# Four-sublayer trunk on one core: the DeltaNet stage with ScalarE and VectorE in program order, later weight splits, and its modulation sums made one stage earlier

## The chip, the core and the metric

One core of a Trainium2 chip runs the whole kernel. Its engines are TensorE (PE in the rows), VectorE (DVE), ScalarE (ACT), GpSimd (POOL) and SyncE (SP), which here only issues DMAs. The metric is the device time of one execution in microseconds (us).

## What is computed

A trunk of four sublayers on x (512 tokens x 1024): a mixer of pooling and sparse attention ("e"), a gated feed-forward with a depthwise convolution ("f"), a gated DeltaNet ("o") and a second feed-forward. Each is wrapped in a modulation from the vector c (shift, scale and gate, each a 1024x1024 matrix times silu(c)) and a post-norm:

```python
def adaln_post_norm(x, c, mod_w, mod_b, ln_g, ln_b, sublayer):
    mod = jax.nn.silu(c) @ mod_w + mod_b
    shift, scale, gate = jnp.split(mod[:, None, :], 3, axis=-1)
    y = sublayer(x * (1.0 + scale) + shift)
    return layer_norm(DEEPNORM_ALPHA * x + gate * y, ln_g, ln_b)
```

The DeltaNet projects to q, k, v, gate, beta and decay, convolves q, k and v over 4 tokens, applies SiLU, normalizes q and k, and solves for each chunk of 64 tokens a triangular system:

```python
    a = jnp.einsum('bhncd,bhnsd->bhncs', kb, k) * dec_strict
    t_mat = lax.linalg.triangular_solve(a + eye, jnp.broadcast_to(eye, a.shape),
                                        left_side=True, lower=True, unit_diagonal=True)
    u = t_mat @ (v * beta[..., None])
    w = t_mat @ (kb * jnp.exp(gc)[..., None])
    attn = jnp.einsum('bhncd,bhnsd->bhncs', q, k) * dec_incl
```

A scan over the chunks, a gated norm and the output projection follow.

## The kernel before

All matrices are float32. A weight tile is split into two fp32r halves (`split`, lines 94 to 99): ScalarE rounds it to the high half (line 97), VectorE or GpSimd subtracts that from the raw tile (line 98). Each product is three matmuls (lines 103 to 105), so one projection of 128 output columns over 1024 inputs is 24 matmuls of 128x512.

The DeltaNet input stage (`odd`) walks over 33 tiles of its input projection: 16 columns for beta and decay, then `ORDER`: g0 to g4, k0 to k7, q0 to q3, g5, q4 to q7, v0 to v7, g6, g7. The generator `projs` yields the result buffer of one tile after the other. It keeps `AHEAD` tiles loaded and split in advance: after tile n's projection it issues load and split of tile n + 3. For each k, q and v tile the stage does a convolution (`conv`: line 1003 on ScalarE, three steps of line 1005 on VectorE) and a SiLU (line 1006), and starts a generator for what follows. `pump` advances every started generator by one step (to its next `yield`):

- `k_chain`: transposes (line 1021), sums of squares (1026), a power on GpSimd (1057), the decayed k (1043), and the block of A (matmul 1050, VectorE 1052), which goes to DRAM.
- `q_chain`: the same squares and power, one step later the scores q k^T (matmul 1076, VectorE 1078, mask on GpSimd 1079).
- `v_chain`: transposes and a product with beta (1065).
- `invert`: inverts all 32x32 diagonal blocks of all heads at once on VectorE. It reads A's blocks back from DRAM, then does 31 steps of a product (line 1096) and a subtraction (1097), a `yield` after every fifth, and a copy (1100), and writes the inverse and its transpose to DRAM (1101, 1102). It starts at q2.
- `y_chain`, four of them, started at the tiles in `YS`: load inverted blocks (1119) and put them together to 64-row inverses (matmuls 1124, 1131, 1139, 1141, 1148).
- `side`: the gate row of this sublayer from its finished sum (`mod_gate`), x times gain plus bias of the previous norm (`affine`, eight GpSimd instructions, lines 506 and 510), and the shift and scale of the next feed-forward (`mod_gb`).

A modulation vector is made by `mod_acc`, not by matmuls: blocks of 128 of the 1024 input rows are loaded (line 267) and added up as row times c, on VectorE (lines 276, 278) or by ScalarE's product and GpSimd's sum (270, 272). `sum_rows` then sums over the partitions (transposes 300, reduction 301). In the DeltaNet stage this is 32 loads of 256 KB, half of them summed on VectorE, half on ScalarE and GpSimd. The gate's sum of the DeltaNet is made in the down phase of the feed-forward before it (`sums`), from 16 such loads.

What sets the order: TensorE's instructions of the input stage stand in program order (`manual_schedule(engines={PE})`). ScalarE, VectorE, GpSimd and SyncE take the order that a list scheduler gives them there, by its own estimate of when operands are ready. `QUIET` names the tiles whose lower weight half VectorE computes instead of GpSimd (q5, q6, q7, v0). PSUM holds four "main" buffers (projections), three "chain" and one "side".

Of the kernel before, what the change touches and what calls it, by code (L numbers as in the profile page):

```python
# [14 lines left out]
P = 128  # L15
S = 512
D = 1024
# [9 lines left out]
class Trunk:  # L27
# [79 lines left out]

    def load_w(self, src, c0, n=P, lo_eng=None, tags=("wh", "wl")):
# [3 lines left out]
        return self.split(raw, [P, KC, n], *tags, lo_eng)  # L112
# [43 lines left out]
    def projs(self, src, tiles, h, start=None, lo_eng=None):  # L156
# [31 lines left out]
        AHEAD = 3 if self.kind == "o" else 2  # L188
        eng = lambda n: lo_eng[n] if isinstance(lo_eng, list) else lo_eng
        ahead = [self.load_w(src, *t, eng(first + n)) for n, t in enumerate(tiles[first:first + AHEAD])]  # L190
        for t, w, p in zip(tiles, ws, pss):
            if start is None:
                self.proj(p[:t[1]], w, h, slice(S // 2, S))
            yield p[:t[1]]
        for n in range(first, len(tiles)):
# [3 lines left out]
            if n + AHEAD < len(tiles):  # L199
                ahead.append(self.load_w(src, *tiles[n + AHEAD], eng(n + AHEAD)))  # L200
# [52 lines left out]
    def mod_acc(self, i, j, tag=None):  # L253
# [6 lines left out]
        acc = self.b("acc", [P, D])  # L260
        for k in range(KC):
            c = self.cs[:, k:k + 1]
            n = D if tag == "g4" else 512
            for q in range(D // n):
                part = acc[:, q * n:(q + 1) * n]
# [14 lines left out]
        return acc  # L280

    def mod_cols(self, i, j):

        nc = self.nc
        acc = yield from self.mod_acc(i, j)
        for _ in range(self.LAG[self.kind]):
            yield
        o = self.s([P, KC], f"modc{j}")
        for q in range(2):
            self.sum_rows(acc[:, q * 512:(q + 1) * 512], o[:, 4 * q:4 * q + 4])  # L290
            yield
# [11 lines left out]
    def mod_gb(self, i):  # L303

        nc = self.nc
        sc = yield from self.mod_cols(i, 1)
        sh = yield from self.mod_cols(i, 0)
# [11 lines left out]
    def mod_gate(self, i, acc=None):  # L319
# [3 lines left out]
        keep = acc is not None  # L323
        if not keep:
            acc = yield from self.mod_acc(i, 2)
        for q in range(2):
            row, part = self.b("mr", [1, 512]), acc[0:1, q * 512:(q + 1) * 512]
# [3 lines left out]
        for h in range(2):  # L331
            part = acc[:, h * 512:(h + 1) * 512]
# [3 lines left out]
            yield  # L336
            p = self.ps("side")
            nc.tensor.matmul(p, self.ones, hi, start=True, stop=False)
            nc.tensor.matmul(p, self.ones, lo, start=False, stop=True)
            if keep:  # L340
                row = self.b("mr", [1, 512])
                nc.scalar.activation(row, p[0:1], AF.Copy)
                nc.sync.dma_start(self.gate_d[:, h * 512:(h + 1) * 512], row)
            else:
                nc.scalar.activation(g[:, h * 512:(h + 1) * 512], p, AF.Copy)
        self.gate = g

    def sums(self, i):

        self.ahead = yield from self.mod_acc(i, 2, "t")  # L350

    def side(self, i):

        if self.ahead is not None:
            yield from self.mod_gate(i, self.ahead)
            self.ahead = None
            yield from self.affine(i)
            if i + 1 < len(self.subs):
                yield from self.mod_gb(i + 1)
# [7 lines left out]
        if i + 1 < len(self.subs):  # L367
            yield from self.mod_gb(i + 1)
# [145 lines left out]
    def ffn(self, i, l, h):  # L514
# [4 lines left out]
        self.go(self.side(i), 2)  # L519
        av = []  # L520
        tiles = self.tiles("f")
        for (c0, _), p in zip(tiles, self.projs(a["f_w_up"][l], tiles, h, self.begin)):
# [7 lines left out]
            if len(av) == 2:  # L530
# [3 lines left out]
                av = []  # L534
                self.pump()
# [10 lines left out]
        if i + 1 < len(self.subs) and self.subs[i + 1][0] == "o":  # L546
            self.go(self.sums(i + 1))
# [335 lines left out]
    def odd(self, i, l, h):  # L883
# [199 lines left out]
        def invert():  # L1083
# [7 lines left out]
            nc.vector.memset(Xs.rearrange("p i j -> p (i j)")[:, ::33], 1.0)  # L1091
            for j in range(31):
# [5 lines left out]
                if j % 5 == 4:  # L1098
                    yield
# [238 lines left out]
```

## Time and profile before

| | us |
|---|---|
| median of 3 runs | 1333.46 (1326.49 to 1335.98) |
| profiled execution | 1331.74 |
| its span, first to last instruction | 1329.6 |
| TensorE busy | 1253.8 (94%) |
| VectorE busy | 835.4 (63%) |
| ScalarE busy | 591.0 (44%) |
| GpSimd busy | 365.2 (27%) |

Mean granted clock of TensorE: 0.971 of full speed. The page's first section gives the busy sums, its second the busy share in 40 slices. A window gives the same for a stretch of time. A row of waits names the instruction that stood, what released it, and how long the engine was idle in all. Times count from the start of the span. The first feed-forward's up phase is about 255 to 505 us, its down phase to 605; the DeltaNet's input stage is about 605 to 881, its recurrence and output projection end at about 1000.

### The profile page before, as it was taken

The page shows a single profiled execution, that of the slowest core. Times are in us where ns is not written, and L with a number is a line of the kernel's source. Part 1 is how long each engine was busy: PE and PEld are TensorE (multiplying, and loading weights), DVE is VectorE, ACT ScalarE, POOL GpSimd, SP SyncE. Part 2 cuts the span into 40 slices and gives each one's busy share as a digit, 9 for nine tenths or more (in the row PEclk, how much of TensorE's full clock was granted, in tenths as well). Part 3 has the DMA queues.
Part 4 walks back from the last instruction along what each step waited for, and adds up shares of the span by engine and source line. Part 5 has one row for each costly group of instructions (what it writes and reads, how often), then busy time and mean ns, then how long its engine had stood idle before and what let it go on. Part 6 is the DMA issues. An engine that isn't in the chain of part 4 may idle for free. (4 is left out here: it accounts for less than half of the span.)

```text
span 1329.6 us, 17388 instructions
## 1 busy us (share of the span) xinstructions
PE 1253.8 (94%) x6359; PEld 1026.5 (77%) x6359; DVE 835.4 (63%) x1388; ACT 591.0 (44%) x1085; POOL 365.2 (27%) x308
## 2 busy tenths in 40 slices
PE   4998899899999999999989987999999999999997
PEld 3756465798888888888878866888798888888885
DVE  4589963476776777445567895537547765556328
ACT  3564756653433343326665434344555343334220
POOL 4367476340100001003585355200380010000001
PEclk9989798999999999999999998999899999999999
DMA  9952444234554536331557537573234643323311
GB/s 265 237 166 88 159 130 140 80 99 158 174 174 145 188 130 203 121 88 33 168 180 215 134 96 204 141 254 115 75 101 141 212 121 96 95 79 111 95 64 64
DMA packets 223626, 184.19 MB, mean 139 GB/s; under 512 B 24735, under 2 KB 191852, under 8 KB 223542
## 3 DMA queue, kind: packets, MB, share of 16 engines
q1 hardware_dynamic: 223542, 183.09, 45.8%
q8 instruction: 50, 0.82, 0.3%
q14 instruction: 34, 0.28, 0.1%
HBM read 169.29 MB, written 13.64 MB: 138 GB/s over the span
## 5 line engine op out<-in xcount | busy, mean ns | idle before, releaser
L103 PE MATMUL main<-h,wh 128*128 128x512 f32 (+2 forms) x1104 | 414.5, 380 | 2.2 <-ACT h L446 2.1
L104 PE MATMUL main<-h,wh 128*128 128x512 f32 (+2 forms) x1104 | 413.2, 375 | 1.9 <-DVE h L394 1.1
L105 PE MATMUL main<-h,wl 128*128 128x512 f32 (+2 forms) x1104 | 412.8, 375 | 0.0
L97 ACT ACTIVATE wh<-wr 128x1024 fp32r<-128x1024 f32 x176 | 184.3, 1050 | 316.0 <-PE main L104 213.5
L98 DVE TENSOR_TENSOR wl<-wr,wh 128x1024 fp32r<-128x1024 f32 x130 | 175.8, 1354 | 176.1 <-ACT wh L97 176.1
L103 PEld LDWEIGHTS main<-h,wh 128*128 128x128 f32 (+1 forms) x1104 | 207.7, 189 | 43.0 <-ACT h L446 2.7
L104 PEld LDWEIGHTS main<-h,wh 128*128 128x128 f32 (+1 forms) x1104 | 208.1, 189 | 40.5 <-DVE h L394 2.0
L105 PEld LDWEIGHTS main<-h,wl 128*128 128x128 f32 (+1 forms) x1104 | 208.0, 188 | 37.4 <-issue 0.4
L527 DVE SCALAR_TENSOR_TENSOR t<-main,cw,t 128x511 f32<-128x511 f32 (+1 forms) x164 | 121.6, 744 | 2.3 <-ACT t L525 0.3
L98 POOL TENSOR_TENSOR wl<-wr,wh 128x1024 fp32r<-128x1024 f32 (+1 forms) x46 | 110.3, 2402 | 45.9 <-ACT wh L97 36.3
L480 POOL TENSOR_TENSOR rstd<-rstd,mhalf 128x1 f32<-128x1 f32 x16 | 10.4, 652 | 363.4 <-DVE rstd L479 333.1
L329 POOL TENSOR_TENSOR acc<-acc,mr 1x512 f32<-1x512 f32 x8 | 12.6, 1582 | 295.8 <-DVE acc L278 222.8
L272 POOL TENSOR_TENSOR acc<-acc,mr 128x512 f32<-128x512 f32 x56 | 74.3, 1329 | 56.3 <-ACT mr L270 53.5
L270 ACT ACTIVATE mr<-mr,cs 128x512 f32<-128x512 f32 x56 | 40.2, 720 | 57.8 <-DMA mr<-in_f_mod_w_dram 39.0
L525 ACT ACTIVATE t<-main,cb,cw 128x512 f32<-128x512 f32 x82 | 62.2, 760 | 0.0
L1005 DVE SCALAR_TENSOR_TENSOR t<-main,ocw,t 128x511 f32<-128x511 f32 (+2 forms) x72 | 53.6, 744 | 3.1 <-ACT t L1003 2.1
L532 ACT ACTIVATE t<-t 128x512 f32<-128x512 f32 x42 | 26.4, 629 | 60.6 <-DVE t L527 60.6
L103 PE MATMUL main<-wh,h 128*128 128x512 f32 x128 | 50.2, 392 | 0.0
L104 PE MATMUL main<-wl,h 128*128 128x512 f32 x128 | 50.1, 391 | 0.0
L105 PE MATMUL main<-wh,h 128*128 128x512 f32 x128 | 49.8, 390 | 0.0
L394 DVE TENSOR_TENSOR h<-chain,h 128x256 fp32r<-128x256 f32 x48 | 19.4, 418 | 30.1 <-ACT h L393 29.6
L390 ACT ACTIVATE chain<-chain,B,G 128x128 f32<-128x128 f32 x84 | 33.2, 435 | 10.0 <-PE chain L382 9.5
(392 smaller groups left out, 2119.4 us busy)
## 6 DMA issues: line engine op xcount, KB each, us to landing
wr<-in_f_w_up_dram SPq DMA_DIRECT2D x84, 512.0 KB
wr<-in_f_w_down_dram SPq DMA_DIRECT2D x42, 512.0 KB
mr<-in_f_mod_w_dram SPq DMA_DIRECT2D x64, 256.0 KB
wr<-in_o_w_in_dram SPq DMA_DIRECT2D x32, 512.0 KB
g<-in_e_mod_w_dram SPq DMA_DIRECT2D x32, 256.0 KB
g<-in_f_mod_w_dram SPq DMA_DIRECT2D x16, 512.0 KB
g<-in_o_mod_w_dram SPq DMA_DIRECT2D x16, 512.0 KB
wr<-in_e_w_in_dram SPq DMA_DIRECT2D x11, 512.0 KB
```

The costliest lines, as they stand in the source:

```text
L97: nc.scalar.activation(hi, src, AF.Copy)
L98: (lo_eng or nc.vector).tensor_tensor(lo, src, hi.bitcast(F32), op=ALU.subtract)
L103: inst = mm(ps, l[0], r[0], start=start, stop=False)
L104: mm(ps, l[0], r[1], start=False, stop=False)
L105: mm(ps, l[1], r[0], start=False, stop=stop)
L270: inst = nc.scalar.activation(r, raw, AF.Copy, scale=c)
L272: nc.gpsimd.tensor_tensor(part, part, r, op=ALU.add)
L390: nc.scalar.activation(t[:, c, :], t[:, c, :], AF.Identity, scale=G[:, k:k + 1], bias=B[:, k:k + 1])
L525: nc.scalar.activation(t, p, AF.Identity, bias=cb[:, n:n + 1], scale=cw[:, 4 * NF + n:4 * NF + n + 1])
L527: nc.vector.scalar_tensor_tensor(t[:, k:], p[:, :S - k], cw[:, 2 * NF * (2 - k) + n:2 * NF * (2 - k) + n + 1], t[:, k:], op0=ALU.mult, op1 ...
L532: nc.scalar.activation(av[0], av[0], AF.Silu)
L1005: nc.vector.scalar_tensor_tensor(t[:, k:], p[:, :S - k], cw[:, 24 * (3 - k) + n:24 * (3 - k) + n + 1], t[:, k:], op0=ALU.mult, op1=ALU.add)
```

## The change

1. In the input stage ScalarE and VectorE are in program order too. GpSimd and SyncE stay with the scheduler.
2. `projs` splits a weight tile one tile later than before, two tiles ahead instead of three, but issues its raw load one tile before the split (`raw_w`).
3. The SiLU of a tile is written after `pump`, except for k0 and k1. Before, it stood ahead of it.
4. `QUIET` is q4 to q7. `YS` is v0, v2, v4, v6, with one more `yield` between the loads and the first matmul of a `y_chain`.
5. `invert` starts at q3 and takes six steps: the setup, then pieces of 10, 7, 7 and 7 inversion steps (the last with the copy), at the pumps of g5, q4, q5 and q6.
6. No modulation sum is left in the stage. The DeltaNet's gate row is finished in the up phase of the feed-forward before (8 more sums of 128x1024, `side` at 2 or 3 steps a pump), and the scale and shift sums of the next feed-forward are made in its down phase (32 loads of 256 KB and 32 sums of 128x512 on VectorE, where 16 stood). In the stage itself `side` only transposes and reduces them at g4, k0, k1 and k2, and does `affine`.

```diff
-    LAG = {"e": 1, "f": 1, "o": 3}
-    QUIET = [("q", 5), ("q", 6), ("q", 7), ("v", 0)]
-    YS = [("v", 1), ("v", 3), ("v", 5), ("v", 6)]
+    QUIET = [("q", 4), ("q", 5), ("q", 6), ("q", 7)]
+    YS = [("v", 0), ("v", 2), ("v", 4), ("v", 6)]
...
-        AHEAD = 3 if self.kind == "o" else 2
+        AHEAD, ROOM = 2, int(self.kind == "o")
         eng = lambda n: lo_eng[n] if isinstance(lo_eng, list) else lo_eng
         ahead = [self.load_w(src, *t, eng(first + n)) for n, t in enumerate(tiles[first:first + AHEAD])]
+        raws = [self.raw_w(src, *t) for t in tiles[first + AHEAD:first + AHEAD + ROOM]]
...
             self.proj(p[:m], ahead.pop(0), h)
-            if n + AHEAD < len(tiles):
-                ahead.append(self.load_w(src, *tiles[n + AHEAD], eng(n + AHEAD)))
+            if n + AHEAD + ROOM < len(tiles):
+                raws.append(self.raw_w(src, *tiles[n + AHEAD + ROOM]))
+            if raws:
+                raw = raws.pop(0)
+                ahead.append(self.split(raw, list(raw.shape), "wh", "wl", eng(n + AHEAD)))
             yield p[:m]
...
-                if kind == "e" or kind == "o" and q:
+                if kind == "e":
                     r = part if k == 0 else raw
                     inst = nc.scalar.activation(r, raw, AF.Copy, scale=c)
...
     def sums(self, i):
 
-        self.ahead = yield from self.mod_acc(i, 2, "t")
+        sc = yield from self.mod_acc(i, 1, "t")
+        sh = yield from self.mod_acc(i, 0, "t", "c")
+        self.ahead = (sh, sc)
 
     def side(self, i):
 
-        if self.ahead is not None:
-            yield from self.mod_gate(i, self.ahead)
-            self.ahead = None
+
+        nxt = i + 1 if i + 1 < len(self.subs) else None
+        if self.subs[i][0] == "o":
+            if nxt is not None:
+                yield from self.mod_gb(nxt, self.ahead)
             yield from self.affine(i)
-            if i + 1 < len(self.subs):
-                yield from self.mod_gb(i + 1)
             self.gate = self.b("gate", [P, D])
...
+        if self.before_o(i):
+            yield from self.mod_gate(nxt, True)
...
-                if j % 5 == 4:
+                if j in (9, 16, 23):
                     yield
...
-        with self.tc.manual_schedule(engines={mybir.EngineType.PE}):
+        todo = []
+        E = mybir.EngineType
+        with self.tc.manual_schedule(engines={E.PE, E.Activation, E.DVE}):
...
                     conv(hd * P, p, qh(hd))
-                    silu()
                     self.go(q_chain(hd))
-                    if hd == 2:
+                    if hd == 3:
                         self.go(invert())
...
                 self.pump()
+                if (kind, hd) not in self.ORDER[5:7]:
+                    silu()
```

Line numbers after the change are higher by 17 in the functions of the stage (1003 is 1020, 1096 is 1114).

Two places of the new order. First ScalarE, before, around the splits for the last q and the first v tiles (L97 is a weight split, L1003 the start of a convolution, L1026 the squares, L1006 the SiLU of the tile whose buffer is named t):

```order
L97 ACTIVATE wh_1234_6732<-wr_1233_6730 128x1024
L1003 ACTIVATE t_1212_6595<-main_1207_6563,ocw_5107 128x512
L1026 ACTIVATE junk_79,ssq_985_5123<-chain_1220_6623 128x128 x4
L97 ACTIVATE wh_1242_6789<-wr_1241_6787 128x1024
L1003 ACTIVATE t_1225_6665<-main_1221_6634,ocw_5107 128x512
L1026 ACTIVATE junk_79,ssq_985_5123<-chain_1231_6694 128x128
L1006 ACTIVATE g4_1211_6594<-t_1212_6595 128x512
L1026 ACTIVATE junk_79,ssq_985_5123<-chain_1231_6694 128x128 x3
L1006 ACTIVATE g4_1211_6594<-t_1225_6665 128x512
L97 ACTIVATE wh_1252_6857<-wr_1251_6855 128x1024
L1003 ACTIVATE t_1236_6736<-main_1232_6705,ocw_5107 128x512
```

And in the change, the same place (L1020, L1043 and L1023 are those lines now; wh_1243 is the weight of v1, wh_1251 that of v2, g4_1231 holds q6 and q7):

```order
L97 ACTIVATE wh_1229_6652<-wr_1214_6583 128x1024
L1020 ACTIVATE t_1232_6657<-main_1227_6625,ocw_5208 128x512
L1043 ACTIVATE junk_79,ssq_1022_5224<-chain_1240_6686 128x128 x4
L1023 ACTIVATE g4_1231_6656<-t_1232_6657 128x512
L97 ACTIVATE wh_1243_6725<-wr_1228_6650 128x1024
L1020 ACTIVATE t_1245_6729<-main_1241_6698,ocw_5208 128x512
L1043 ACTIVATE junk_79,ssq_1022_5224<-chain_1248_6744 128x128 x4
L1023 ACTIVATE g4_1231_6656<-t_1245_6729 128x512
L97 ACTIVATE wh_1251_6783<-wr_1242_6723 128x1024
L1020 ACTIVATE t_1253_6787<-main_1249_6756,ocw_5208 128x512
L1043 ACTIVATE junk_79,ssq_1022_5224<-chain_1256_6801 128x128 x4
```

Before, the split wh_1242 stood ahead of the SiLU of t_1212, whose convolution had been started earlier; now each split stands behind the SiLU of the tile before.

Second, VectorE, before, near the end of the inversion (L1096 and L1097 the inversion, L1005 a convolution, L1056 the input of a power):

```order
L1096 TENSOR_TENSOR c_1215_6608<-xn_1140_6237,xn_1141_6238 128x156
L1005 SCALAR_TENSOR_TENSOR t_1225_6665<-main_1221_6634,ocw_5107,t_1225_6665 128x510
L1097 TENSOR_TENSOR xn_1141_6238<-xn_1141_6238,c_1215_6608 128x6x26
L1056 TENSOR_SCALAR fq_990_5128<-ssq_985_5123 128x4
L1005 SCALAR_TENSOR_TENSOR t_1225_6665<-main_1221_6634,ocw_5107,t_1225_6665 128x509
L1096 TENSOR_TENSOR c_1216_6611<-xn_1140_6237,xn_1141_6238 128x135
L1097 TENSOR_TENSOR xn_1141_6238<-xn_1141_6238,c_1216_6611 128x5x27
L1096 TENSOR_TENSOR c_1217_6614<-xn_1140_6237,xn_1141_6238 128x112
L1097 TENSOR_TENSOR xn_1141_6238<-xn_1141_6238,c_1217_6614 128x4x28
L1096 TENSOR_TENSOR c_1218_6617<-xn_1140_6237,xn_1141_6238 128x87
L1097 TENSOR_TENSOR xn_1141_6238<-xn_1141_6238,c_1218_6617 128x3x29
L1096 TENSOR_TENSOR c_1219_6620<-xn_1140_6237,xn_1141_6238 128x60
```

And in the change, at its end (L1115 the inversion's last subtraction, L1118 the copy, L1022 the convolutions of q7 and then v0, L1095 the scores of q4):

```order
L1114 TENSOR_TENSOR c_1238_6677<-xn_1177_6386,xn_1178_6387 128x60
L1115 TENSOR_TENSOR xn_1178_6387<-xn_1178_6387,c_1238_6677 128x2x30
L1114 TENSOR_TENSOR c_1239_6680<-xn_1177_6386,xn_1178_6387 128x31
L1115 TENSOR_TENSOR xn_1178_6387<-xn_1178_6387,c_1239_6680 128x31
L1118 COPY xn_1177_6386<-xn_1178_6387 128x1024
L1073 TENSOR_SCALAR fq_1027_5229<-ssq_1022_5224 128x4
L1022 SCALAR_TENSOR_TENSOR t_1245_6729<-main_1241_6698,ocw_5208,t_1245_6729 128x511
L1022 SCALAR_TENSOR_TENSOR t_1245_6729<-main_1241_6698,ocw_5208,t_1245_6729 128x510
L1022 SCALAR_TENSOR_TENSOR t_1245_6729<-main_1241_6698,ocw_5208,t_1245_6729 128x509
L1206 SCALAR_TENSOR_TENSOR c2_1024_5226<-br2_1025_5227,ex_1020_5222 128x32
L1095 TENSOR_TENSOR c_1247_6740<-chain_1246_6735,g4_1034_5243 128x512
L1073 TENSOR_SCALAR fq_1027_5229<-ssq_1022_5224 128x4
```

Before, the steps of a convolution lie between single inversion instructions; now a whole piece with the copy stands ahead of q7's convolution, and the scores of q4 behind that.

## Rows read from the trace of the kernel before

**Rows 1.** Section 2 of the page: TensorE, busy tenths in 40 slices of 33.24 us.
```profile
PE   4998899899999999999989987999999999999997
```
**Rows 2.** Windows, feed-forward stage before: start:end us, length, busy us and instructions by engine.
```profile
260.00:500.00 240.00, 240.00 (x1178) 203.44 (x1178) 167.33 (x205) 101.47 (x137) 26.26 (x15) 1.00 0.46 150
505.00:600.00 95.00, 95.00 (x425) 78.78 (x424) 48.43 (x55) 30.97 (x39) 6.74 (x5) 1.00 0.42 127
```
**Rows 3.** Waits of TensorE, 640 to 884 us: line, releaser, us, times, longest.
```profile
PE side L300 <- DVE modc L301: 4.7, 1, 4.7
PE chain L1021 <- ACT junk L1026: 4.5, 2, 3.9
PE chain L1124 <- issue: 4.0, 1, 4.0
PE chain L1050 <- DVE rk L1056: 3.3, 1, 3.3
PE chain L1076 <- DVE c L1078: 1.8, 2, 1.2
PE chain L1021 <- DVE g L1052: 1.3, 1, 1.3
```
**Rows 4.** Windows of 10 us in the DeltaNet input stage (after POOL: clock, DMA share, GB/s).
```profile
690.00:700.00 10.00, 7.25 (x35) 6.68 (x36) 9.51 (x22) 5.49 (x19) 7.42 (x9) 0.83 0.73 218
760.00:770.00 10.00, 10.00 (x47) 8.28 (x46) 9.77 (x17) 2.15 (x3) 5.04 (x3) 1.00 0.30 82
770.00:780.00 10.00, 6.06 (x27) 5.04 (x26) 9.70 (x19) 5.29 (x15) 4.25 (x3) 0.83 0.38 103
800.00:810.00 10.00, 5.27 (x30) 5.13 (x29) 7.71 (x14) 4.19 (x12) 7.85 (x6) 0.66 1.00 201
830.00:840.00 10.00, 10.00 (x38) 8.45 (x38) 4.13 (x5) 2.56 (x4) 4.94 (x4) 0.67 0.69 185
```
**Rows 5.** Groups by line, 640 to 884 us: instructions, busy, mean ns, idle before.
```profile
L278 DVE SCALAR_TENSOR_TENSOR acc<-mr,cs,acc 128x512 f32<-128x512 f32 x14 | 16.6, 1189 | 29.5 <-DMA mr<-in_f_mod_w_dram 29.4
L270 ACT ACTIVATE mr<-mr,cs 128x512 f32<-128x512 f32 x14 | 10.1, 722 | 31.3 <-DMA mr<-in_f_mod_w_dram 25.2 <-DVE t L1005 3.4 <-DMA g<-xt_d 2.7
```
**Rows 6.** Timeline of VectorE: start us, us, instruction.
```profile
756.87 2.47 DVE L1097 TENSOR_TENSOR xn<-xn,c 128x231 f32<-128x231 f32 x1
763.28 0.42 DVE L1097 TENSOR_TENSOR xn<-xn,c 128x252 f32<-128x252 f32 x1
```
**Rows 7.** Timeline of GpSimd: start us, us, instruction, idle before.
```profile
663.57 7.11 POOL L510 TENSOR_TENSOR x<-x,acc 128x1024 f32<-128x1024 f32 x3 [4.67 <-DMA acc<-in_f_ln_b_dram]
...
756.54 2.54 POOL L98 TENSOR_TENSOR wl<-wr,wh 128x1024 fp32r<-128x1024 f32 x1
```
**Rows 8.** Timeline of ScalarE, the SiLU of q5.
```profile
771.80 0.63 ACT L1006 ACTIVATE g<-t 128x512 f32<-128x512 f32 x1 [7.14 <-DVE t L1005]
```
**Rows 9.** Groups of VectorE by line, 738 to 800 us.
```profile
L1096 DVE TENSOR_TENSOR c<-xn,xn 128x31 f32<-128x31 f32 (+15 forms) x31 | 16.8, 541 | 4.3 <-DMA xn<-a_d 3.4
L1097 DVE TENSOR_TENSOR xn<-xn,c 128x31 f32<-128x31 f32 (+15 forms) x31 | 16.7, 538 | 0.7
L1005 DVE SCALAR_TENSOR_TENSOR t<-main,ocw,t 128x509 f32<-128x509 f32 (+2 forms) x20 | 14.9, 747 | 1.8 <-ACT t L1003 1.6
L1078 DVE TENSOR_TENSOR c<-chain,g 128x512 f32<-128x512 f32 x7 | 4.8, 682 | 0.0
L1100 DVE COPY xn<-xn 128x1024 f32<-128x1024 f32 x1 | 1.7, 1687 | 0.0
```
**Rows 10.** Timeline of TensorE: first matmul of g5 and of q4.
```profile
739.00 0.48 PE L103 MATMUL main<-h,wh 128*128 128x512 f32 x1
...
745.81 0.48 PE L103 MATMUL main<-h,wh 128*128 128x512 f32 x1
```
**Rows 11.** Line 278: its instructions, ns least, median and most.
```profile
L278 DVE SCALAR_TENSOR_TENSOR acc<-g,cs,acc x28: 1270/1277/1286, 324.4 to 1066.7; 128x1024 f32<-128x1024 f32 x28
L278 DVE SCALAR_TENSOR_TENSOR acc<-t,cs,acc x14: 739/745/752, 497.3 to 516.8; 128x512 f32<-128x512 f32 x14
```

More of the change, by code (lines that the diff above doesn't have):

```diff
@@ L259, in mod_acc @@
         tag = tag or ("g4" if kind == "f" else "mr")
-        acc = self.b("acc", [P, D])
+        if into == "acc":
+            acc = self.b("acc", [P, D])
+            parts = [acc[:, q * 512:(q + 1) * 512] for q in range(2)]
+        else:
+            parts = [self.b(into, [P, 512]) for _ in range(2)]
         for k in range(KC):
             c = self.cs[:, k:k + 1]
-            n = D if tag == "g4" else 512
-            for q in range(D // n):
-                part = acc[:, q * n:(q + 1) * n]
+            whole = tag == "g4"
+            for q, part in enumerate([acc] if whole else parts):
+                n = D if whole else 512
                 raw = self.b(tag, [P, n])
                 nc.sync.dma_start(raw, w[k * P:(k + 1) * P, j * D + q * n:j * D + (q + 1) * n])
-                if kind == "e" or kind == "o" and q:
+                if kind == "e":
                     r = part if k == 0 else raw
@@ L279, in mod_acc, with mod_cols @@
             yield
-        return acc
-    def mod_cols(self, i, j):
+        return parts
+    def mod_cols(self, i, j, parts=None):
         nc = self.nc
-        acc = yield from self.mod_acc(i, j)
-        for _ in range(self.LAG[self.kind]):
+        if parts is None:
+            parts = yield from self.mod_acc(i, j)
             yield
@@ L317, in mod_gb, with mod_gate @@
         self.GB = (G, B)
-    def mod_gate(self, i, acc=None):
+    def mod_gate(self, i, keep=False):
         nc = self.nc
         kind, l = self.subs[i]
-        keep = acc is not None
-        if not keep:
-            acc = yield from self.mod_acc(i, 2)
+        parts = yield from self.mod_acc(i, 2)
         for q in range(2):
-            row, part = self.b("mr", [1, 512]), acc[0:1, q * 512:(q + 1) * 512]
+            row, part = self.b("mr", [1, 512]), parts[q][0:1]
             nc.sync.dma_start(row, self.a[kind + "_mod_b"][l:l + 1, 2 * D + q * 512:2 * D + (q + 1) * 512])
@@ L330, in mod_gate @@
         g = None if keep else self.b("gate", [P, D])
-        for h in range(2):
-            part = acc[:, h * 512:(h + 1) * 512]
+        for q, part in enumerate(parts):
             hi, lo = self.b("mr", [P, 512], F32R), self.b("mr", [P, 512], F32R)
@@ L366, in side @@
             self.params()
-        if i + 1 < len(self.subs):
-            yield from self.mod_gb(i + 1)
+        if nxt is not None:
+            yield from self.mod_gb(nxt)
+        if self.before_o(i):
+            yield from self.mod_gate(nxt, True)
     def new_h(self):
@@ L545, in ffn @@
         late = []
-        if i + 1 < len(self.subs) and self.subs[i + 1][0] == "o":
-            self.go(self.sums(i + 1))
+        if self.before_o(i) and i + 2 < len(self.subs):
+            self.go(self.sums(i + 2))
         for j in range(len(gs)):
```

44 lines of the change are left out of this document (23 added, 21 removed).

## The prediction

> **What bounds the kernel now.** I read the page's 40 slices first, then the waits of TensorE, then the windows around each wait, then the timelines of VectorE and GpSimd. The reader is to see in the slices that TensorE is at nine tenths or more nearly everywhere, and that outside the first stage it falls to eight and seven tenths only in slices 21, 24 and 25 (665 to 698 and 765 to 831 us) [rows 1]. In the windows both feed-forward stages have TensorE busy for every microsecond: 240.00 of 240 in the up phase before the DeltaNet stage, 95.00 of 95 in its down phase, at clock 1.00, with VectorE at 167 of 240 and 48 of 95 [rows 2]. There only more TensorE work, or a partner that becomes late, changes the time. The DeltaNet input stage (640 to 884 us) is different: TensorE waits there for 19.6 us in the eight waits of the six kinds shown, and for about 1 us in smaller ones [rows 3]. After the long ones the granted clock of the 10 us window is 0.83, 0.83, 0.66 and 0.67 [rows 4], so part of it ran at 1.2 instead of 2.4 GHz. The shortfall from 1 times 10 us is 1.7, 1.7, 3.4 and 3.3 us; a part of the third falls into the wait itself, so I count 9 us. What the stage can give back in all is thus 20 + 9, about 29 us.
>
> **The change, part by part.** I take it as four terms against the profiled execution's own 1331.74 us (its span is 1329.6).
>
> *Term A, the k heads: -5.5.* The waits of 3.3 us (a squared-norm scale that came late, behind ScalarE's work on modulation loads) and 1.3 us, and the clock of 690 to 700 (1.7 us) belong here [rows 3, 4]. The 16 modulation products on ScalarE and their adds on GpSimd leave the stage: 14 instructions of 0.72 us with 31 us of idle before them stand in one group [rows 5]. With them go the waits, since ScalarE now keeps program order, and ahead of the squares it has a weight split and a convolution start, no modulation work. That returns 6.3. What can be late instead: the weight halves of k3 and k4 are still split on GpSimd, behind three products x times gain that take 7.1 us and start only when a norm row has landed [rows 7]. There I allow 0 to 2 us and take 0.8.
>
> *Term B, the matrix inversion and the q heads: +4.* Here I count the row of VectorE by hand from the end of q3's projection (t = 0). A tile costs TensorE 6.81 us (from one first matmul to the next) [rows 10]; so without waits it would have q7 done at 33, v0 at 40, v1 at 46 and v2 at 53. VectorE's row, now in fixed order, is from t = 9.8 (first inversion piece, once the conv of q3 and a split are done): the 62 inversion instructions, 33.5 us in two groups [rows 9], less what seven of them were held, five at about 2.4 instead of 0.4 and two at 1.3 (one of the seven and a clean one are shown [rows 6]), so 22.5; the closing copy, 1.7 [rows 9]; convolutions of q4 to q7, 12 at 0.75, 9.0 [rows 9]; two weight splits, at 1.3 by the same 128x1024 row, 2.6; three score products at 0.68, 2.0 [rows 9]; and holds. An inversion instruction that meets a GpSimd split waits it out: the 128x231 subtract took 2.47 us where the 128x252 one took 0.42, and a GpSimd split ran from 756.54 to 759.08 [rows 6, 7]. In the new order two such splits (v0, v1) and one or two of GpSimd's mask products still fall beside inversion pieces: 6 us. Sum 44; so q4's score product is done near t = 55.
>
> The Trainium skill, page "SBUF — State Buffer", section "Who interferes with whom", says this as a rule: a VectorE instruction with two SBUF inputs and a GpSimd instruction that reads SBUF exclude each other for a whole instruction. The trace agrees, 2.47 against 0.42 us. By that rule moving four splits to VectorE removes holds, and it speaks against leaving v0's and v1's splits on GpSimd.
>
> TensorE against that: q7 ends at 33 as before. v0's lower half is split by GpSimd at 36, a wait of 2.4; v0 ends at 41.5. Its pump then needs a score buffer whose squares stand on ScalarE behind the SiLU of q6, which waits for q6's convolution (t = 44, behind the third inversion piece): TensorE goes on at about 47, 5.8 later. v1 follows, and v2 needs the split that stands on ScalarE behind the SiLU of q7, whose convolution is only through at 54.8, so v2 starts at 59 and ends at 65 to 66 (some 3 us of clock loss lie inside it). Before, VectorE was equally full (9.7 of 10 in 760 to 780 us [rows 4]), ScalarE waited 7.14 us for a convolution there [rows 8], and TensorE lost 4.5 + 1.8 us in waits and 1.7 in clock [rows 3, 4], 8 us, which puts the end of v2 at t = 53 + 8 = 61. So this term is a loss of 4 to 5; I take 4. Its bounds are -6 (the lag of VectorE is swallowed by the two tiles that are split ahead) and +12 (every one of v0 to v2 waits in full, at the low clock).
>
> *Term C, the v and gate heads: -13.* The waits of 4.7 (transposes of a sum whose reduction came last) and 4.0 us (triangular products whose inputs SyncE issued late, behind modulation loads) stand here, with clocks 0.66 and 0.67 [rows 3, 4]. All 32 modulation loads, 8 MB, leave the stage, as do 14 VectorE sums that idled 29.5 us for them [rows 5]. 8.7 us of waits and 5.6 of clock go: 14.3. What comes in place: the loads of the inverse's blocks now stand on SyncE behind the store of q5's scores, which by the row above is ready only near t = 62, when TensorE wants them at 65. I allow 0 to 5 and take 1.3, nearer to nothing, since the 3 us between 62 and 65 are there for the load.
>
> *Term D, the feed-forward stage before: +0.5.* It gets 8 more sums of 1.28 us in its up phase and 16 more of 0.74 in its down phase [rows 11]: 10 us to VectorE's 167 of 240 and 12 to its 48 of 95 [rows 2]. Both stay under TensorE, which hides them, and the loads, 8 MB more, meet a DMA share of 0.46 and 0.42 [rows 2]. If that cover fails (a weight split behind two sums) it costs one sum at a time; bounds 0 to 5, and I take 0.5. The recurrence and everything after it keep their order.
>
> Sum: -5.5 + 4 - 13 + 0.5 = -14, so 1331.7 - 14 = 1317.7, say 1318 us. The profiled execution lies 1.7 below the median of the three runs, inside their spread of 9.5; I leave the forecast on its scale.
>
> **The rivals.**
>
> *Everything comes back.* Split-ahead tiles and the four main result buffers swallow VectorE's lag. For it: TensorE was at 10.00 of 10 in 760 to 770 us while VectorE was already at 9.77 [rows 4], so a lag of a tile or so costs nothing. Against it: 22 us of lag (55 - 33) is three tiles, and only two are split ahead. With B at -6, C at -14 and D at 0 it gives 1306.
>
> *Program order eats it.* Term B at +12 and the late blocks at 5 us: -5.5 + 12 - 9 + 0.5 = -2, so 1330, no change that a measurement of this kernel can tell; about 1% is what it can. For it: in fixed order a SiLU that waits blocks the next weight split, which the scheduler was free to put first (in the rows of ScalarE's order above it does so once).
>
> *Slower.* The same mechanism without slack: every split of q6 to v2 stands behind a SiLU that stands behind an inversion piece, so that TensorE pays VectorE's full row from q4 on, 44 us over four tiles or 11 for one, instead of 6.81 [rows 10]. The lag of 22 us (55 - 33) turns into waits at four or five places, each with a clock loss of 1.7 to 3.4 [rows 4], about 10 more; less the 8 lost there before that is +24, and with A only half found and D at +5 the sum is -3 + 24 - 9 + 5 = +17, 1349. It decides from the point where q6's projection already waits for its split. Against it: q4 to q7 are split by VectorE right between the pieces, not after them.
>
> **How the numbers follow.** Forecast (1309 to 1324) 0.5; everything back 0.15; eaten 0.25; slower 0.1. The forecast lies close to the bound of 1% (1320), so 0.37 of its 0.5 counts as faster and 0.13 as the same: with the others faster 0.52, same 0.38, slower 0.1. The range takes in the first rival and most of the second: 1304 to 1338.
>
> **What would show it right or wrong.** In the stage's waits of TensorE the kinds of 4.7, 4.0 and 3.3 us should be gone; there should be no modulation loads or sums between 640 and 880. A new wait of 4 to 7 us should stand at v0's pump, for ScalarE's squares, and one of 2 to 4 before v2's projection, for a split. VectorE should be above nine tenths for some 45 us from q4 to v0, and the closing copy should end near 52 us after q3's projection. The feed-forward stage should stay at 100% of TensorE. If v0 and v1 pass without those waits, B is wrong and the first rival holds; if TensorE waits for splits as early as q6, the third; if the feed-forward stage shows idle time, D is.

## The result and the profile after

The changed kernel takes 1317.62 us in the median of 4 runs (1314.80 to 1322.84), the kernel before beside it 1331.92 us (4 runs, 1326.49 to 1335.98). The ratio is 0.99, with a 95% interval of 0.985 to 0.9949. The forecast was 1318. The profiled execution of the changed kernel is the longest of its four, 1322.84 us with a span of 1320.8, so the two traces lie 8.8 us apart and the medians 14.3.

The page's slices of the changed kernel, TensorE and its granted clock:

```profile
PE   4998999899999999999999989999999999999997
PEclk9999598999999999999999999989899999999998
```

Slices 21 and 25, at eight and seven tenths before [rows 1], are at nine; slice 24 is still at eight. The waits of TensorE in the changed kernel, 640 to 900 us (line, releaser: us, times, longest):

```profile
PE chain L1038 <- ACT junk L1043: 4.6, 1, 4.6
PE chain L1038 <- ACT g L1023: 1.8, 1, 1.8
PE main L105 <- DVE wl L98: 1.7, 1, 1.7
PE chain L1038 <- DVE c L1060: 1.1, 1, 1.1
...
PE main L105 <- POOL wl L98: 0.6, 1, 0.6
```

The kinds of 4.7, 4.0 and 3.3 us [rows 3] are gone. The first row is new, though its line is the second one of [rows 3]: the transposes at v0's pump, released by ScalarE's squares (L1043). Its surroundings, three windows of 10 us:

```profile
770.00:780.00 10.00, 9.01 (x45) 7.56 (x46) 9.69 (x13) 3.52 (x11) 3.91 (x2) 1.00 0.37 93
780.00:790.00 10.00, 5.42 (x28) 4.61 (x27) 9.44 (x19) 3.51 (x11) 2.35 (x1) 0.89 0.13 38
790.00:800.00 10.00, 9.48 (x38) 7.37 (x36) 8.22 (x18) 4.28 (x13) 5.58 (x4) 0.77 1.04 236
```

VectorE is full (9.69, 9.44), ScalarE a third busy, TensorE at 5.42, and the clock falls to 0.77 behind the wait. What ScalarE did is in its timeline (start us, us, instruction, idle before):

```profile
784.94 0.63 ACT L1023 ACTIVATE g<-t 128x512 f32<-128x512 f32 x1 [8.07 <-DVE t L1022]
785.47 1.04 ACT L97 ACTIVATE wh<-wr 128x1024 fp32r<-128x1024 f32 x1
```

It stood 8.07 us at q6's SiLU, until VectorE had done q6's convolution, and the weight split of v1 and the squares stand behind it. And VectorE, in the same stretch:

```profile
775.56 2.47 DVE L1114 TENSOR_TENSOR c<-xn,xn 128x247 f32<-128x247 f32 x1
778.06 0.42 DVE L1115 TENSOR_TENSOR xn<-xn,c 128x247 f32<-128x247 f32 x1
...
786.27 0.30 DVE L1114 TENSOR_TENSOR c<-xn,xn 128x135 f32<-128x135 f32 x1
786.61 2.48 DVE L1115 TENSOR_TENSOR xn<-xn,c 128x135 f32<-128x135 f32 x1
```

GpSimd beside it, in its own timeline:

```profile
775.21 2.54 POOL L98 TENSOR_TENSOR wl<-wr,wh 128x1024 fp32r<-128x1024 f32 x1
786.59 2.35 POOL L98 TENSOR_TENSOR wl<-wr,wh 128x1024 fp32r<-128x1024 f32 x1 [8.84 <-ACT wh L97]
```

The two inversion instructions of 2.47 and 2.48 us (their partners of the same size take 0.42 and 0.30) are the two that fell beside GpSimd's splits of v0 and v1.

To see where time went, I cut both traces at the same six places of TensorE's timeline. The first is where the feed-forward before ends: the product of the stage's first tile that waits for the last block of its input h. Then come the first matmul of g4's projection, the last of q3's, of v2's and of g7's (for these three, start plus length is the cut), and a product early in the scan, the first that waits for ScalarE. Rows of TensorE's timeline in the changed kernel:

```profile
614.90 0.29 PE L104 MATMUL main<-h,wh 128*16 128x256 f32 x1 [0.79 <-DVE h L409]
...
647.58 0.40 PE L103 MATMUL main<-h,wh 128*128 128x512 f32 x1
...
741.22 0.39 PE L105 MATMUL main<-h,wl 128*128 128x512 f32 x1
...
805.00 0.39 PE L105 MATMUL main<-h,wl 128*128 128x512 f32 x1
...
866.31 0.39 PE L105 MATMUL main<-h,wl 128*128 128x512 f32 x1
...
880.02 0.49 PE L1260 MATMUL main<-c,h 128*128 128x128 f32 x2 [0.69 <-ACT c L1255]
```

Before, the same places are at 610.85, 640.46, 737.91, 799.71, 878.23 and 888.07. The lengths between them, for these two traces and for those of the experiments below (us; the sum is that of the rounded pieces):

| kernel | start | g4 to q3 | g5 to v2 | v3 to g7 | to the scan | sum | median of runs |
|---|---|---|---|---|---|---|---|
| before | 29.6 | 97.4 | 61.8 | 78.5 | 9.8 | 277.1 | 1331.92 |
| changed | 32.7 | 94.0 | 63.8 | 61.3 | 13.3 | 265.1 | 1317.62 |
| sums alone | 29.6 | 90.7 | 60.3 | 71.3 | 9.6 | 261.5 | 1313.97 |
| order alone | 32.7 | 95.1 | 73.4 | 95.3 | 12.2 | 308.7 | 1358.05 |
| late SiLU | 32.7 | 94.0 | 63.8 | 62.8 | 10.2 | 263.5 | 1316.22 |
| six quiet splits | 31.2 | 94.0 | 61.8 | 61.0 | 10.2 | 258.2 | 1307.51 |
| ScalarE free | 29.6 | 99.3 | 71.9 | 61.1 | 10.2 | 272.1 | 1324.33 |
| VectorE free | 32.7 | 90.7 | 63.3 | 67.0 | 10.2 | 263.9 | 1316.69 |
| both free | 29.6 | 90.7 | 63.5 | 68.8 | 10.4 | 263.0 | 1311.12 |
| six quiet, late SiLU | 31.2 | 94.0 | 63.2 | 64.7 | 10.7 | 263.8 | 1314.57 |
| two orders | 29.6 | 90.7 | 61.7 | 61.1 | 10.6 | 253.7 | 1304.56 |
| bare loads | 29.6 | 90.7 | 60.3 | 72.0 | 9.5 | 262.1 | 1315.26 |
| five pieces | 29.6 | 90.7 | 61.4 | 67.4 | 10.7 | 259.8 | 1308.08 |

So the change shortens the stage by 12.0 us in its trace. The feed-forward before it is 1.0 longer (359.8 instead of 358.8 us, from the transposes at its start to the first row above), the first stage ended 3.1 us later in that execution (on this see the last section), and what follows the scan's first products is 0.8 shorter. Together these give the 8.8 us between the two traces.

### The profile page after: what moved, and what is told of

It is laid out like the page before. It is cut to its first block, busy times and chain, and to the rows that moved or that the text cites. A ratio compares the mean times of both kernels' runs of the same rounds, so it can differ in the third digit from the quotient of the medians.

```text
span 1320.8 us, 17326 instructions
## 1 busy us (share of the span) xinstructions
PE 1254.3 (95%) x6359; PEld 1025.2 (78%) x6359; DVE 826.9 (63%) x1396; ACT 583.5 (44%) x1069; POOL 342.6 (26%) x294
## 4 chain that ended last, share of the span: by engine, by line
PE 72%; DVE 12%; DMA 6%; ACT 4%; POOL 3%; issue 2%; SPq 1%; DVEq 0%; POOLq 0%; ACTq 0%
PE main L103 18%; PE main L104 18%; PE main L105 18%; PE chain L104 2%; PE chain L105 2%; PE chain L103 2%; DMA g<-in_e_mod_w_dram 1%; DVE wl L98 1%; PE side L103 1%; DVE g L716 1%; PE side L105 1%; PE side L104 1%; DVE m L715 1%; DMA mr<-in_f_mod_w_dram 1%; DVE xn L1115 1%
## 5 line engine op out<-in xcount | busy, mean ns | idle before, releaser
L97 ACT ACTIVATE wh<-wr 128x1024 fp32r<-128x1024 f32 x176 | 184.0, 1049 | 280.6 <-PE main L104 192.9
L98 DVE TENSOR_TENSOR wl<-wr,wh 128x1024 fp32r<-128x1024 f32 x130 | 172.9, 1332 | 166.8 <-ACT wh L97 166.8
L495 POOL TENSOR_TENSOR rstd<-rstd,mhalf 128x1 f32<-128x1 f32 x16 | 10.4, 651 | 395.1 <-DVE rstd L494 364.9
L1022 DVE SCALAR_TENSOR_TENSOR t<-main,ocw,t 128x511 f32<-128x511 f32 (+2 forms) x72 | 53.9, 748 | 57.5 <-ACT t L1020 55.8
L282 POOL TENSOR_TENSOR acc<-acc,mr 128x512 f32<-128x512 f32 x42 | 55.2, 1321 | 33.7 <-ACT mr L280 30.7
L288 DVE SCALAR_TENSOR_TENSOR acc<-g,cs,acc 128x1024 f32<-128x1024 f32 x35 | 44.7, 1277 | 0.3
L280 ACT ACTIVATE mr<-mr,cs 128x512 f32<-128x512 f32 x42 | 30.1, 720 | 25.7 <-DMA mr<-in_f_mod_w_dram 12.9
```

Source lines behind the costliest of these rows:

```text
L97: nc.scalar.activation(hi, src, AF.Copy)
L98: (lo_eng or nc.vector).tensor_tensor(lo, src, hi.bitcast(F32), op=ALU.subtract)
L280: inst = nc.scalar.activation(r, raw, AF.Copy, scale=c)
L282: nc.gpsimd.tensor_tensor(part, part, r, op=ALU.add)
L288: nc.vector.scalar_tensor_tensor(part, raw, c, part, op0=ALU.mult, op1=ALU.add)
L1022: nc.vector.scalar_tensor_tensor(t[:, k:], p[:, :S - k], cw[:, 24 * (3 - k) + n:24 * (3 - k) + n + 1], t[:, k:], op0=ALU.mult, op1=ALU.add)
```

## The experiments

The kernel before ran beside every group, at medians of 1328.8 to 1329.9 us; ratios are to these.

### The sums alone, and the order alone

The first takes the kernel before and applies part 6 of the change; the second applies parts 1 to 5. The second so keeps `side` as it was, with its 32 loads, and has the line of the three engines; the first keeps TensorE's order alone, and has of the change:

```diff
         if self.subs[i][0] == "o":
+            if nxt is not None:
+                yield from self.mod_gb(nxt, self.ahead)
             yield from self.affine(i)
-            if i + 1 < len(self.subs):
-                yield from self.mod_gb(i + 1)
```

Expected of the sums alone:

> The kernel before with part 6 of the change alone: all modulation sums leave the DeltaNet stage, order of ScalarE and VectorE, splits, SiLU, inversion and y chains as before. Theory S (the gain is the modulation loads and sums that leave the stage): the waits of 4.7, 4.0 and 3.3 us and their clock loss go, 12 to 18 us under the kernel before, 1314 to 1320 us, about the changed kernel. Theory O (the gain is the fixed order and the inversion in pieces): at most 5 us under the kernel before, 1327 or more.

Expected of the order alone:

> The kernel before with parts 1 to 5 alone; the 32 modulation loads and their sums stay in the stage, now also in program order on ScalarE and VectorE. Theory S: no gain, 1328 to 1345 us, since in-order engines wait for the loads and everything behind them waits too. Theory O: 1318 to 1323 us.

Measured, for the sums alone 1313.97 us, ratio 0.9876 (0.9846 to 0.9907); the order alone 1358.05 us, ratio 1.0209 (1.0179 to 1.0238). Theory S holds, Theory O falls: without the moved sums the fixed order is 2% slower than the kernel before, well beyond what was expected. The longest waits of TensorE with the order alone, 640 to 905 us:

```profile
PE chain L1134 <- issue: 9.4, 1, 9.4
PE chain L1134 <- DVE c L1073: 7.9, 1, 7.9
PE main L105 <- DVE wl L98: 7.2, 2, 6.7
PE chain L1029 <- ACT junk L1034: 7.1, 2, 6.3
```

TensorE's waits about double. The first two rows are the second and third y chain, and just before each of these waits ended VectorE had stood for a modulation load (4.68 and 3.74 us), with a v head's product with beta (L1073) behind it in order; TensorE went on within about 0.1 us of that product's end. The longest of the other two rows lie at q7 and between v0 and v1, beside the inversion. The sums alone are not slower than the whole change, so what the runs gain is part 6's; parts 1 to 5 add nothing that the runs show. But the sums alone bring only 7.2 us in the v part (78.5 to 71.3), and there a wait stands that the kernel before did not show. TensorE's longest waits with the sums alone:

```profile
PE chain L1135 <- DMA g<-xt_d: 5.7, 1, 5.7
```

This is the first product of the first y chain, waiting for blocks of the inverse. Before, the wait for the modulation reduction, 4.7 us, stood just ahead of that product, which then had no wait of its own. (The 4.0 us on the same line in [rows 3] are the second y chain's, at 829.50, and are gone with the sums alone.)

### Which engine's order

Each is the changed kernel with one or two engines given back to the scheduler in the input stage: ScalarE (the edit shown), VectorE (`{E.PE, E.Activation}`), or both (`{E.PE}`).

```diff
-        with self.tc.manual_schedule(engines={E.PE, E.Activation, E.DVE}):
+        with self.tc.manual_schedule(engines={E.PE, E.DVE}):
```

> The changed kernel with ScalarE's order in the input stage left to the scheduler again; VectorE stays in program order. Theory A (ScalarE's fixed order costs the k heads 3 us, the wait of 1.8 us for a SiLU and a slower walk, and the stage's start 1.5 us): 3 to 6 us under the changed kernel, and the piece from g4 to the end of q3 takes about 91 us instead of 94.0. Rival D (VectorE's order costs them): no difference there, within 2 us of the changed kernel.

> The changed kernel with VectorE's order in the input stage left to the scheduler again; ScalarE stays in program order. Theory A: the piece from g4 to the end of q3 stays at 94 us; near the inversion the convolutions move between its steps again, so the wait at v0's pump for ScalarE's squares shrinks below 4.6 us, but the inversion and with it the blocks for the y chains end later: within 4 us of the changed kernel. Rival D: that piece falls to 91 us, 3 us or more under the changed kernel.

> The changed kernel with only TensorE in program order, as before; inversion in pieces, later splits, later SiLU in the program text, y chains a tile earlier and moved sums stay. If the fixed order of ScalarE and VectorE brings anything by itself, slower than the changed kernel by 3 us or more; if it only costs, 3 to 8 us under it, as the run with the sums alone.

Measured: ScalarE free 1324.33 us, 0.9966 (0.9939 to 0.9993); VectorE free 1316.69, 0.9889 (0.9829 to 0.9949); both free 1311.12, 0.9856 (0.9788 to 0.9924). Theory A falls for the k heads: with ScalarE free they take 99.3 us, longer than before, and rival D's piece is right, 90.7 with VectorE free. Theory A's other half holds: the start is 29.6 wherever ScalarE is free. Rival D's time for the whole (3 us or more gained) isn't there, because the v part grows by 5.7. TensorE's longest waits with ScalarE free:

```profile
PE chain L1038 <- ACT g L1023: 11.1, 3, 6.6
```

The wait now is for the SiLU itself (L1023), three times: once at the k heads, 3.4 us, and twice around v0 and v1. And its longest with VectorE free:

```profile
PE chain L1038 <- DVE c L1095: 7.7, 1, 7.7
PE chain L1143 <- DMA g<-xt_d: 4.2, 1, 4.2
```

The blocks of the inverse are late again (second row), as with the sums alone. The inversion's closing copy starts, counted from the end of q3's projection, at 791.3 - 741.6 = 49.7 us in the changed kernel and at 792.2 - 734.7 = 57.5 with VectorE free. But with ScalarE free and VectorE fixed it starts no earlier, at 790.8 - 732.6 = 58.2. The copies, first of the changed kernel, then with VectorE free, then with ScalarE free:

```profile
L1118 DVE COPY xn<-xn x1: 1084/1084/1084, 791.3 to 791.3; 128x1024 f32<-128x1024 f32 x1
```

```profile
L1118 DVE COPY xn<-xn x1: 1714/1714/1714, 792.2 to 792.2; 128x1024 f32<-128x1024 f32 x1
```

```profile
L1118 DVE COPY xn<-xn x1: 1082/1082/1082, 790.8 to 790.8; 128x1024 f32<-128x1024 f32 x1
```

So beside a fixed ScalarE, VectorE's fixed order costs 3.3 us at the k heads and ends the inversion some 8 us earlier; the v heads are then 5.7 us shorter. It takes both orders: ScalarE's costs 1.6 to 3.1 at the start, and beside a fixed VectorE it saves 5.3 us at the k heads and 8.1 from g5 to v2. How much of the 8 us is the order itself isn't shown. The inversion's 62 instructions are busy for 27.5 us in the changed kernel, 31.9 with VectorE free, 35.8 with ScalarE free and 35.3 with both free, so in these runs more of them were held, and GpSimd, beside which they are held, is in the scheduler's order everywhere.

By the runs alone none of the three is told from the changed kernel, since their intervals overlap its own; the pieces of the traces tell them apart. Both free is 6.5 us under the changed kernel by the medians, as expected if the fixed order only costs, and 2.1 by the pieces.

### ScalarE's queue or VectorE's row

The wait of 4.6 us stands on ScalarE. Two edits of the changed kernel ask whether ScalarE's queue or what it waits for makes it: the SiLU of q4 to v1 one tile later, the lower halves of v0 and v1 on VectorE, and both.

```diff
                 self.pump()
+                wait = (kind, hd) in self.ORDER[18:24]
+                if wait:
+                    prior.append(late.pop())
+                    late[:] = prior[:-1]
+                    del prior[:-1]
+                elif prior:
+                    late[:0] = prior
+                    prior.clear()
                 if (kind, hd) not in self.ORDER[5:7]:
                     silu()
```

```diff
-    QUIET = [("q", 4), ("q", 5), ("q", 6), ("q", 7)]
+    QUIET = [("q", 4), ("q", 5), ("q", 6), ("q", 7), ("v", 0), ("v", 1)]
```

> The changed kernel with the SiLU of q4 to v1 written one tile later, so that on ScalarE the next weight split, the next convolution start and the squares stand ahead of it. Theory Q (TensorE's wait of 4.6 us at v0's pump is head-of-line blocking on ScalarE): that wait and the low clock of v1 and v2 behind it (2.4 and 0.9 us) go, 5 to 8 us under the changed kernel. Theory V (VectorE's row of work is the bound, ScalarE only passes it on): the wait stands again at the same or the next tile, released by VectorE, and the time is within 2 us of the changed kernel.

> The changed kernel with the lower weight halves of v0 and v1 computed on VectorE too, in place of GpSimd. By the lock of VectorE and GpSimd: VectorE gets 2 x 1.3 us more work and loses two holds of some 2 us, so its row is 1 us shorter or equal, and the split itself is done 1 us earlier: 0 to 3 us under the changed kernel. If holds are not what fills the row: 2 to 4 us over it.

> The changed kernel with both of the edits tried before: lower halves of v0 and v1 on VectorE, and the SiLU of q4 to v1 one tile later. If the two losses are separate (a lock, and ScalarE's queue): 1 to 4 us under the run with the six splits on VectorE alone. If VectorE's row is the one bound: the same as that run within 2 us.

Measured: late SiLU 1316.22 us, 0.9887 (0.9853 to 0.992); six quiet splits 1307.51, 0.9828 (0.9796 to 0.9859); both 1314.57, 0.9878 (0.9833 to 0.9923). Theory Q falls. With the late SiLU the piece g5 to v2 has the same 63.8 us, and of TensorE's longest waits two are VectorE's, 3.8 and 2.9 us:

```profile
PE main L105 <- DVE wl L98: 3.8, 1, 3.8
PE chain L1038 <- DVE fq L1073: 2.9, 1, 2.9
```

ScalarE only passed the wait on, as Theory V says. With six quiet splits the piece is 2.0 us shorter, and the wait for the squares is gone, but a wait for VectorE's splits takes its place, here as a row of TensorE's waits:

```profile
PE main L105 <- DVE wl L98: 5.7, 3, 3.7
```

The 2.0 us fit VectorE's row: the inversion's instructions are busy for 23.2 us instead of 27.5, and two splits of 1.22 us come to it. The stage is 6.9 us shorter than the changed kernel's by the sum in the table, but only 2.0 of it in this piece. The start and the piece to the scan, which the edit does not touch, give 1.5 and 3.1: in the changed kernel's trace both ran partly at the low clock. Its windows of the two pieces (the third number from the end is the clock):

```profile
866.70:880.00 13.30, 11.93 (x120) 10.90 (x120) 3.40 (x5) 4.75 (x9) 0.00 (x0) 0.74 0.85 314
615.00:647.60 32.60, 31.09 (x249) 29.93 (x249) 10.05 (x35) 16.27 (x33) 12.60 (x7) 0.95 0.20 63
```

With the late SiLU the first of them has clock 1.00, with six quiet splits the second:

```profile
862.80:873.00 10.20, 8.85 (x121) 8.13 (x120) 3.40 (x5) 4.78 (x9) 0.00 (x0) 1.00 0.98 357
```

```profile
605.00:636.20 31.20, 29.68 (x249) 28.52 (x250) 10.14 (x36) 16.39 (x33) 12.62 (x7) 1.00 0.22 69
```

The runs say 10 us for the edit; by the traces 2 of them are shown. Both edits together make the stage 5.6 us longer than the splits alone, so the two losses aren't separate; neither expectation had it slower, and why it is stays open.

### Two orders in one stage, and shorter pieces

The pieces say that the scheduler's order is better up to q3 and the program's from g5 on. The loop is cut there, with the six quiet splits:

```diff
+        with self.tc.manual_schedule(engines={E.PE}):
+            for kind, hd in self.ORDER[:17]:
...
+        with self.tc.manual_schedule(engines={E.PE, E.Activation, E.DVE}):
+            for kind, hd in self.ORDER[17:]:
```

> The changed kernel with v0's and v1's lower halves on VectorE too, and with ScalarE and VectorE in the scheduler's order up to q3 and in program order from g5 on. If the pieces of the stage add up as their traces say (start 29.6 and k heads 90.7 us with the scheduler's order, inversion 61.8 and v heads 61.0 us with the fixed order and six quiet splits): stage 5 us shorter than with six quiet splits alone, about 1302 to 1305 us. If the seam costs what it brings (the scheduler places work of the first half without knowing the second): 1307 us or more.

Measured: 1304.56 us, 0.9813 (0.9783 to 0.9842). Each piece came out as the one that it was taken from: 29.6, 90.7, 61.7, 61.1. It has the lowest median of this study, and its interval lies below that of the changed kernel (which begins at 0.985), as it does below 1; some of the other experiments' intervals overlap it. What is left is TensorE's longest wait, for splits in VectorE's row of work:

```profile
PE main L105 <- DVE wl L98: 5.6, 3, 3.8
```

Then the inversion in five pieces, so that none is longer than a tile:

```diff
-                if j in (9, 16, 23):
+                if j in (8, 13, 18, 24):
```

> The kernel with two orders, and the inversion in five pieces (9, 5, 5, 6 and 6 steps and the copy, at the pumps of g5, q4, q5, q6 and q7) instead of four. If TensorE's waits of 5.6 us for a weight half from VectorE come from pieces that are longer than a tile: they fall to 3 us or less, with the low clock behind them, 3 to 6 us under the kernel with two orders. If the whole row of VectorE is the bound, the waits move to v1 and the blocks for the y chains come late: within 2 us of it or slower.

Measured: 1308.08 us, 0.9843 (0.9808 to 0.9878). The waits for splits fell to 2.7, and others came in their place, in TensorE's waits:

```profile
PE chain L1143 <- DMA g<-xt_d: 3.3, 1, 3.3
PE main L105 <- DVE wl L98: 2.7, 2, 1.4
```

The blocks are late by 3.3 us and the v part takes 67.4 instead of 61.1. That is what was expected if VectorE's whole row is the bound: cutting it finer moves the wait.

### Loads that nobody reads

> The kernel with the sums alone moved out, and with 32 loads of 256 KB put back into the input stage (2 at each tile from k2 on), which nothing reads: the traffic and the DMA issues of the modulation sums without their work on VectorE, ScalarE and GpSimd. Theory T (the loads themselves, by traffic and SyncE's queue, cost the waits): most of the gain is lost, 1325 us or more, and y's block loads come late again. Theory W (the waits came from engines that stood for loads and from what stood behind them): within 4 us of the kernel with the sums moved out, 1311 to 1318 us.

```diff
+                        raw = self.b("mr", [P, 512])
+                        inst = nc.sync.dma_start(raw, wm[lm][k * P:(k + 1) * P, j * D + q * 512:j * D + (q + 1) * 512])
+                        self.after(inst, self.cv)
```

The 32 loads are extra, their result is used by nothing. Measured: 1315.26 us, 0.9905 (0.9871 to 0.994), and a stage of 262.1 us against 261.5 without them. Theory W fits: 8 MB more traffic and 32 more issues cost the stage 0.6 us. But the bare loads were issued from 657.8 to 766.0 us, all ahead of the y chains, while in the kernel before half of the 32 were issued from 806.8 us on; and no sum holds their buffers, where before SyncE waited 10.6 us for VectorE's sums (L278) and 10.4 for GpSimd's (L272) before it could issue such a load. So the test speaks for the k and q heads, and not for the v heads or for a SyncE that stands.

For the v heads the trace of the kernel before shows what stood, at the wait of 4.0 us in [rows 3]. Rows of SyncE's, ScalarE's and TensorE's timelines:

```profile
813.50 1.86 SPq L1119 DMA_DIRECT2D g<-xt_d  x4
```

```profile
826.16 0.72 ACT L270 ACTIVATE mr<-mr,cs 128x512 f32<-128x512 f32 x1 [7.16 <-DMA mr<-in_f_mod_w_dram]
...
828.82 0.58 ACT L1143 ACTIVATE c<-chain 64x512 f32<-64x512 f32 x1
```

```profile
829.50 0.71 PE L1124 MATMUL chain<-g,g 128*128 128x64 f32 x3 [3.96 <-issue]
```

The product's blocks were issued some 14 us before it started, and their packets in the trace are done by 816.5 us. ScalarE stood 7.16 us for a modulation load, with a copy of the first y chain (L1143) behind it, and the product starts 0.1 us after that copy's end. This fits a product that waits for the copy to free one of the three chain buffers; the profile names no releaser. Here, then, the cost of the modulation sums is an engine that stands for a load with other work behind it.

## Why the prediction was right, and where it wasn't

The time, 1318 against 1317.62, is right, and so is the mechanism as a whole: the modulation sums leave the stage, VectorE's row around the inversion takes some of the gain back. The terms are less good than their sum.

*Term A, -5.5.* Measured -3.4 (97.4 to 94.0). The step that failed is "with them go the waits, since ScalarE now keeps program order". The waits go with the sums alone, -6.7 (90.7), with the scheduler's order; VectorE's fixed order then takes 3.3 back, in a wait of 1.8 us for a SiLU and one of 1.1 for the decayed k. What I allowed for instead, the weight halves of k3 and k4 behind GpSimd's products, shows no wait.

*Not in the sum: the start, +3.1.* I took the stage from its k heads on. ScalarE's fixed order also holds its first tiles: the copy of the beta and decay columns (L1181) stands behind weight splits, TensorE waits 1.5 us for it, and about as much is the low clock of that piece (31.2 instead of 32.7 us where the clock stayed at 1.00). The piece takes 29.6 us, as before, in every trace with ScalarE free there.

*Term B, +4.* Measured +2.0. The count by hand held well (its row, 9.8 and 44, makes 53.8 and not 55; q4's score product ended at 53.7): v0's projection ended at 783.13 - 741.61 = 41.5 us (41.5 counted), the wait at its pump was 4.6 (5.8), the copy ended at 50.8 (52), v2 at 63.8 (65 to 66). The sentence "the trace agrees" on the exclusion of VectorE and GpSimd is borne out by two more such instructions, 2.47 and 2.48 us. The wait of 2.4 that I gave v0 stood at q7, 1.7 us, for VectorE's own split. The wait of 2 to 4 us expected before v2 was 0.6, and VectorE was above nine tenths for 30 us (760 to 790) and not for 45. That ScalarE's queue makes the wait, as I put it, is only where it shows: the late SiLU gives the same length.

*Term C, -13.* Measured -17.2 to g7, and +3.5 from there to the scan, together -13.7. Of the 3.5, 3.1 are not the change's: the kernels built on it need 10.2 to 10.7 us there, and this one trace had a clock of 0.74. The size was close, but the step "triangular products whose inputs SyncE issued late, behind modulation loads" failed: they were issued 14 us ahead, and ScalarE was what stood for a modulation load (7.16 us, rows above). Nor do the waits simply go with the sums. With the sums gone and the order as before, the first y chain waits 5.7 us for the inverse and the v part gains only 7.2. In the changed kernel the blocks come without a wait (I took 1.3), and there the inversion ends some 8 us earlier. Of the 17.2, then, 7.2 come with the sums alone (78.5 to 71.3), 2.5 more with parts 2 to 5 under the scheduler's order (68.8), and 7.5 with the two fixed orders, which I had put into term B alone, as a cost.

*Term D, +0.5.* Measured +1.0, but not told from chance: the piece takes 358.3 us in three and 359.8 or 359.9 in eight of the eleven traces with the moved sums, and 358.8 in the two traces without. TensorE was busy for 100.00 of 100 us in a window of the down phase:

```profile
500.00:600.00 100.00, 100.00 (x448) 82.88 (x446) 62.13 (x79) 27.97 (x31) 1.10 (x2) 1.00 0.59 187
```

VectorE has 62.13 us of work in this window of the changed kernel, and a DMA share of 0.59, more than the rows of before show for the stretch [rows 2], all of it under TensorE, as forecast.

By the terms' own traces the sum is 3.1 - 3.4 + 2.0 - 17.2 + 3.5 + 1.0 = -11.0; the runs' medians say -14.3. That the forecast of -14 meets the latter to half a microsecond is partly luck.

## What to carry to other kernels

Here a fixed order of both engines paid where one engine's long row (the inversion) had to end early for others, and cost where short work of several engines interleaves. Cut a stage where the better of the two changes, and add up the pieces of the traces before running it. Moving work out of a stage uncovers the wait that stood behind it: look for what is needed next after each wait that you remove. When a wait is put down to an engine that is a third busy, ask what that engine stood for: reordering its queue gave nothing here, while taking two holds by GpSimd off the full engine gave 2.0 us.

## What was not expected

The first stage is the same in the changed kernel and the eight kernels built on it (TensorE's instructions stand there in one and the same order), but it ended at different times in their traces: TensorE's transposes after its norm came at 243.3 to 255.1 us. Two of them, the changed kernel and the one with two orders:

```profile
255.06 0.77 PE L397 MATMUL chain<-ident,x 128*128 128x128 f32 x3 [1.26 <-DVE h L409]
```

```profile
243.35 0.66 PE L397 MATMUL chain<-ident,x 128*128 128x128 f32 x4 [1.22 <-DVE h L409]
```

That is 12 us, more than the term that most experiments were to show, while the later stage's pieces repeat closely where the clock is the same (90.7 in six traces). A good part is TensorE's clock. Windows of the same two kernels:

```profile
150.00:200.00 50.00, 50.00 (x234) 33.34 (x232) 32.37 (x91) 28.16 (x65) 28.07 (x27) 0.87 0.37 107
```

```profile
150.00:200.00 50.00, 49.81 (x263) 33.22 (x263) 35.61 (x101) 32.19 (x74) 33.43 (x33) 1.00 0.44 132
```

TensorE is busy for nearly all of both, but gets through 234 and 263 instructions, at clock 0.87 and 1.00. Why the clock differs wasn't tried. The variation is why the kernels here are compared by pieces of the stage, and why a single run of them tells little below 1%.

VectorE in program order beside a ScalarE that the scheduler orders was worse than either order for both: 99.3 us for the k heads, where both fixed took 94.0 and both free 90.7.
